# Five buffers for value tiles, table products inside the block loop, a later token row, and another split of the fill steps in a hybrid encoder layer

## The chip, the cores and the metric

The kernel runs on one core of a Trainium2 chip. The metric is device time in microseconds (us) of one execution. The engines are named as in the profile: PE (TensorE, matmuls), DVE (VectorE), ACT (ScalarE), POOL (GpSimd) and SP, whose queue issues every DMA of this kernel. Each engine works through its own list of instructions in order and waits where an operand or a buffer is not ready.

## The reference

One layer of a bidirectional encoder on 1024 tokens of width 1024, fp32. An input projection of the RMS-normed tokens gives latents for a multi-head latent attention (8 heads), q, k and v of a dilated attention (24 heads of 64 in three groups with window and dilation (128,1), (512,4), (2048,16)), two gating inputs and two merge gates:

```
h = rmsnorm(x); proj = h @ w_in
c_q, c_kv, k_rope, z_mla, q_dil, k_dil, v_dil, z_dil, g_mla, g_dil = split(proj)
a_out = mla_attention(rmsnorm(c_q) @ w_uq, rmsnorm(c_kv) @ w_ukv, rope(k_rope))
outs, lses = dilated_group(rope(q_dil), rope(k_dil), v_dil)   # per group
d_out = sum(softmax(lses over the groups) * outs)
y_mla = (a_out * silu(z_mla)) @ w_o_mla;  y_dil = (d_out * silu(z_dil)) @ w_o_dil
x = x + (sigmoid(g_mla + b) * y_mla + sigmoid(g_dil + b) * y_dil) @ w_out
return rmsnorm(x, final_norm_g)
```

## The kernel before

Every product is made in three matmuls, `mm3`: each fp32 operand is split into a high part (`w_h`, a cast on ACT, L150) and the remainder (`w_l`, a subtraction on POOL or DVE, L151), and L144 to L146 add high x high, high x low and low x high. The tokens stay unnormed; the factor 1/rms of each token is multiplied in later, either by partition (`rcol`, a column per 128 tokens) or along the free axis (`R`, a row of 1024 factors that is broadcast to 128 partitions through a DRAM tensor, `s_rs`).

The stages, by the trace:

- 0 to 226 us, in an order that a list scheduler makes: projection of the latents, tables of cosines and sines (`cos_d` and `sin_d` for the dilated heads, tile name `cs_d`), the token factors (`token_factors`: squares, inverse root, `rcol`, and the row `R` by a transpose on PE, L279, and two DMAs), the latents' up-projection (`latents`, whose scaling L357 on DVE comes before PE's transposes L364, whose results ACT empties into `lat_h`, L367, from a ring of two PSUM banks), and the values of the dilated heads (`dil_v`, three groups by two halves, 8 token tiles of 24 matmuls each). `dil_v` takes a tile from PSUM in a high part on ACT (L445) and a low part on DVE (L446) into the SBUF tile `dv_st`, and stores it to `s_dv`; the ring of `dv_st` has three buffers, so the fourth tile waits for the first store to land. Among this runs the loading of up-projection weights: `u_raw`, one buffer, which is cast on ACT into `uq_h` and split on POOL into `uq_l` in two portions, so the second portion's load waits for the first portion's split.
- 226 to 531 us, `blocks`: 16 items of 7 products of 12 matmuls, in an order written out by hand (Strassen-like combinations of half blocks). In each step `x`, operands of the product five places ahead (LEAD) are cast and split, on POOL among others, and each finished item is rotated with `cos_d` and `sin_d` (L549) and stored as q or k of the dilated heads.
- 531 to 828 us, the dilated attention, a hand-written loop over 72 units and some ends (`attention`). Four pairs of heads have 18 units each: 8 units of group 0, 8 of group 1, and 2 *class units* of group 2 (its dilation makes 16 classes of 64 tokens). One pass of the loop is called a tick below: transposes of unit t (L1144, or L1248 for class units), scores of unit t+2 (L1120, L1121; L1231), ACT's cast of the transposed probabilities (L1152) and DVE's low part (L1156), maxima (L1130), exponentials (L1137), and the values of unit t-1 (L1168, L1175; L1262). Twice in a tick `feed(DIL_FEED[g])` adds to a count of owed steps and issues one *fill* step for each whole step owed: a step is three matmuls of 512 columns of other projections (gates and z, 16 tiles in two halves of 8 steps). When a half is complete its epilogue (L728 on DVE, L730 or L734 on ACT, L731 and L732 on POOL, stores to `s_zs` and `s_gt`) and the split of the next weights follow. The keys and queries of a head are loaded (`at_r<-s_dk`, `at_r<-s_dq`) when the units of two heads before are through.
- After each pair, `combine` weighs the three groups by their softmax denominators: a chain of small operations, much of it on POOL (L1410, L1418, L1421, L1422, L1428), then the spreading of the weights by DMA (`at_f<-s_rr`). It runs in the ticks of the next pair, and SP issues these loads ahead of later heads' keys.
- 828 to 1125 us the latent attention, with the rest of the fill; then the output projection.

In a tick the order is: transposes, scores, casts, then the first feed, earlier results, the second feed, values:

```
            do(t, 3)
            do(t + 2, 0)
...
            self.feed(DIL_FEED[g])
            do(t - 2, 6)
            do(t + 2, 2)
            do(t - 2, 7)
...
            self.feed(DIL_FEED[g])
            do(t - 1, 5)
```

Of the kernel before, what the change touches and what calls it, by code (L numbers as in the profile page):

```python
# [10 lines left out]
F32 = mybir.dt.float32  # L11
F32R = mybir.dt.float32r
I32 = mybir.dt.int32
AF = mybir.ActivationFunctionType
ALU = mybir.AluOpType
# [13 lines left out]


FIRST_FEED = 9
DIL_FEED = (1.33, 1.33, 2.3, 1.8)

LAST_JOBS = [(dt, 0) for dt in range(4)] + [(dt + i, half) for dt in (4, 6) for half in range(2) for i in range(2)] + [(dt, 1) for dt in range(4)]
LAST_STEPS = {3: 4, 4: 6, 5: 8, 6: 9, 8: 14, 9: 15, 10: 17, 11: 19, 12: 20}
# [25 lines left out]
class Net:  # L61
# [203 lines left out]
            if half == 0:  # L265
                v.tensor_scalar(out=self.hb, in0=self.hb, scalar1=0.5, scalar2=None, op0=ALU.mult)

    def token_factors(self, xp, pp):

        nc, a = self.nc, self.a  # L270
        ss = xp.tile([128, 8], F32, name="x_ss", bufs=1)
        for t in range(8):
            x = xp.tile([128, D], F32, name="x_in")
            self.dma(x, a["x"][128 * t:128 * t + 128, :])
            nc.scalar.activation(out=x, in_=x, func=AF.Square, accum_out=ss[:, t:t + 1])
        y = self.rsqrt(ss, 1.0 / D, xp, 8)
        nc.vector.tensor_copy(self.rcol, y)
        pt = pp.tile([128, 512], F32, name="pj")
        nc.tensor.transpose(pt[:8, :128], y, self.ident)  # L279
        row = xp.tile([8, 128], F32, name="x_row", bufs=1)  # L280
        nc.vector.tensor_copy(row, pt[:8, :128])
        self.dma(self.rs, row)
        flat = self.rs.rearrange("a b -> (a b)")
        self.dma(self.R, flat.partition_broadcast(128))
# [137 lines left out]
    def dil_v(self, g, quad, tp, pj):  # L422

        nc, a = self.nc, self.a
        w = []
        for kk in range(2):
            raw = self.wp.tile([128, 4, 256], F32, name="w_raw")
            self.dma(raw, a["wv"][g * 2 + quad, kk])
            for k in range(0, 4, 2):
                wp = (self.wp, self.wpx)[kk]  # L430
                h = wp.tile([128, 2, 256], F32R, name="w_h", bufs=4)
                l = wp.tile([128, 2, 256], F32R, name="w_l", bufs=4)
                self.split(raw[:, k:k + 2], h, l, nc.gpsimd)
                w.append((h, l))
        for t in range(8):
            ps = pj.tile([128, 512], F32, name="pj")[:, :256]
            for kc in range(8):
                wh, wl = w[kc // 2]
                sl = slice(128 * t, 128 * t + 128)
                self.mm3(ps, self.hTh[:, kc, sl], self.hTl[:, kc, sl], wh[:, kc % 2], wl[:, kc % 2], kc == 0, kc == 7)  # L440
            pv = ps.rearrange("p (h d) -> p h d", d=64)
            f = self.rcol[:, t:t + 1]
            if g < 2:
                st = tp.tile([128, 4, 2, 64], F32R, name="dv_st")
                nc.scalar.mul(st[:, :, 0], pv, f)  # L445
                nc.vector.scalar_tensor_tensor(out=st[:, :, 1], in0=pv, scalar=f, in1=st[:, :, 0].bitcast(F32), op0=ALU.mult, op1=ALU.subtract)  # L446
                x = slice(quad * 512, quad * 512 + 512)
                if g == 0:
                    dst = self.dv[0][128 * t + 64:128 * t + 192, x]
                else:  # L450

                    dst = self.dv[1].rearrange("(r m) x -> m r x", r=4)[32 * t:32 * t + 32, :, x]
                self.dma(dst, st.rearrange("p h a d -> p (h a d)"))
            else:
                st = tp.tile([128, 4, 64], F32, name="dv_s2")
                nc.scalar.mul(st, pv, f)
                self.dma(self.dv[2][2 * quad:2 * quad + 2, 128 * t:128 * t + 128].rearrange("a t x -> t a x"), st.rearrange("p (a h) d -> p a (h d)", h=2))
# [191 lines left out]
    def blocks(self, items, tp, pp):  # L649

        self.blk, self.opd = {}, {}
        self.raw_pools = (self.wp, tp)
        self.s = [(h, l) for h, l in zip(self.sh, self.sl)]
        places = 7 * len(items)
        steps, ps = {}, {}
        for n in range(2):
            self.block_loads(n, items[n])
        for i in range(4):
            self.dma(self.dq[2][i].rearrange("e c r h (a b) f m -> (e c r) (h a) (b f m)", a=2), self.zero.unsqueeze(1).to_broadcast([128, 4, 512]))
        for j in range(LEAD):  # L660
            self.block_minus(j, items)
            self.block_operand(j, items)
        self.block_minus(LEAD, items)
        with self.tc.manual_schedule():
            for x in range(1, places + 14):
                n, k = divmod(x - 1, 7)
                j = x - 1
                if j < places:
                    if k == 0:
                        ps[n] = {c: pp.tile([128, 512], F32, name=f"st_{c}{n % 2}") for c in "abcd"}  # L670
                        steps[n] = self.block_steps(n, items[n], ps[n], tp)
                    self.block_product(j, ps[n])
                todo = []

                for m, y in ((n, k + 1), (n - 1, k + 8)):
                    if m in steps:
                        todo += steps[m].pop(y, [])
                for f in todo:
                    f()
                self.block_operand(j + LEAD, items)  # L680
                self.block_minus(j + LEAD + 1, items)

                if x == places - 1:
                    self.close_sums()
                    self.open_areas(0)
                    for load in self.items[0][:2]:
                        load()

                if j == places - 9:
                    self.weights_load(0)  # L690
                    self.weights_load(1)
                if j == places - 3:
                    self.weights_split(0)
                if k == 2 and n + 2 < len(items):
                    self.block_loads(n + 2, items[n + 2])
# [875 lines left out]
    def run(self):  # L1571
        tc, nc = self.tc, self.nc
        with ExitStack() as ctx:
# [28 lines left out]
            with tc.tile_pool(name="wpx", reuse_waits="tile", bufs=2, side="right") as self.wpx, tc.tile_pool(name="cosd", reuse_waits="tile", bufs=1, side="right") as dpool, ExitStack() as sums:  # L1602
                with tc.tile_pool(name="pj_a", reuse_waits="tile", bufs=NB_A, space=PSUM) as pj, tc.tile_pool(name="dvp", reuse_waits="tile", bufs=3, side="right") as vp:
                    with tc.tile_pool(name="lp", reuse_waits="tile", bufs=1) as lp, tc.tile_pool(name="pj_l", reuse_waits="tile", bufs=8 - NB_A, space=PSUM) as pl:
                        with tc.tile_pool(name="wl", reuse_waits="tile", bufs=1) as wl, tc.tile_pool(name="xp", reuse_waits="tile", bufs=3) as xp:
                            self.latent_proj(lp, wl, xp, pj)
                            self.tables(xp)
                            self.token_factors(xp, pl)
                            m = cp.tile([128, 896], F32, name="masks")
                            for x, y, n in ((0, 1024, 256), (256, 896, 128), (384, 256, 512)):  # L1610
                                self.dma(m[:, x:x + n], self.a["masks"][:, y:y + n])

                            self.mask0 = m[:, 64:320], m[:, 384:640], m[:, 640:896]
                            self.mask1 = m[:, 128:384], m[:, 0:256]
                        with tc.tile_pool(name="cosm", reuse_waits="tile", bufs=1) as mpool, tc.tile_pool(name="up", reuse_waits="tile", bufs=1) as lp:
                            self.cos_m, self.sin_m = self.table(mpool, "cs_m", 32)
                            self.cos_d, self.sin_d = self.table(dpool, "cs_d", 0)
                            up = self.up_weights(lp)
                            with tc.tile_pool(name="lt", reuse_waits="tile", bufs=2) as tp:
                                self.latents(up, lp, tp, pl)  # L1620
                            self.dil_v(0, 0, vp, pj)
                            self.dil_v(0, 1, vp, pj)
# [4 lines left out]
                    with tc.tile_pool(name="bs", reuse_waits="tile", bufs=1) as tp:  # L1627
                        self.block_sums(sp, tp)
                        self.dil_v(1, 0, vp, pj)
                    for g, quad in ((1, 1), (2, 0), (2, 1)):  # L1630
                        self.dil_v(g, quad, vp, pj)
                    for x in (self.cos_d, self.sin_d):
                        for half in range(2):
                            c = slice(512 * half, 512 * half + 512)
                            nc.gpsimd.tensor_tensor(out=x[:, c], in0=x[:, c], in1=self.R[:, c], op=ALU.mult)
                    for r in (0, S + 64):
                        for p in range(2):
                            self.dma(self.dk[0][:, p, :, :, r:r + 64].rearrange("h c x t -> (c x) h t"), z[:64].rearrange("p (h t) -> p h t", t=64))
# [8 lines left out]
            pp = ctx.enter_context(tc.tile_pool(name="banks", reuse_waits="tile", bufs=1, space=PSUM))  # L1647
# [95 lines left out]
```

## Time and profile before

Three runs took 1252.14, 1256.94 and 1256.76 us, median 1256.76. The profiled execution took 1254.46 us, and its span in the trace is 1252.5 us.

| engine | busy us | share of the span |
|---|---|---|
| PE | 1212.4 | 97% |
| DVE | 730.8 | 58% |
| ACT | 622.0 | 50% |
| POOL | 570.2 | 46% |

A row of PE's waits names what waited (engine, tile, line), what ended it, the sum in us, how often, and the longest. A row of the table by stretches gives for each engine, in the order PE, PEld (weight loads), DVE, ACT and POOL, the busy us and the instructions, then the clock that PE was granted (1.00 is full), the share of the 16 DMA engines, and GB/s. A row of the timeline is start, duration, engine, line, operation, result<-operands, count; in brackets the idle time before it and what ended it. DMA issues have size and median us from issue to landing.

### The profile page before, as it was taken

To read this page: it belongs to the slowest core of one execution; us is meant where nothing else is said; L and a number is where in the kernel's file an instruction comes from. 1 tells how busy PE (TensorE), PEld (TensorE's weight loads), DVE (VectorE), ACT (ScalarE), POOL (GpSimd) and SP (SyncE) were. 2 spreads that over 40 slices of the span, in tenths; PEclk is the share of its full clock that TensorE was granted. 3 is DMA by queue.
4 is the path that set the end of the run, shared out by engine and by line. 5 is a ranking of instruction groups with operands and counts; after the bars stand their busy time and mean duration, and the time that the engine had idled before them with its cause. 6 is when DMAs were issued, how large, how long until landed. Compare 5 with 4: busy or idle time off the path is not lost.

```text
span 1252.5 us, 19486 instructions
## 1 busy us (share of the span) xinstructions
PE 1212.4 (97%) x6909; PEld 1064.5 (85%) x6909; DVE 730.8 (58%) x1304; ACT 622.0 (50%) x1300; POOL 570.2 (46%) x482
## 2 busy tenths in 40 slices
PE   8979999999999999999999999999999999999998
PEld 8979999888888888888888889878878888888886
DVE  7473534467657653345555575647766767759542
ACT  6534345444343344455554666545655656654232
POOL 2352218877777777543464442415521201168322
PEclk9989999999999999999999999899999999999999
DMA  9847589365445642496887898964634445225241
GB/s 333 225 157 283 196 302 317 103 180 156 135 132 165 174 127 100 122 268 197 233 257 200 207 294 212 266 175 116 178 128 119 110 118 135 85 96 182 84 151 51
DMA packets 126416, 221.37 MB, mean 177 GB/s; under 512 B 28072, under 2 KB 60400, under 8 KB 121392
## 3 DMA queue, kind: packets, MB, share of 16 engines
q1 hardware_dynamic: 126320, 220.14, 59.5%
q8 instruction: 54, 0.88, 0.3%
q14 instruction: 42, 0.34, 0.1%
HBM read 149.24 MB, written 70.85 MB: 176 GB/s over the span
## 4 chain that ended last, share of the span: by engine, by line
PE 75%; DMA 11%; DVE 4%; ACT 4%; issue 3%; POOL 1%; SPq 1%; ACTq 0%; POOLq 0%; DVEq 0%
PE bank L145 5%; PE bank L144 5%; PE bank L146 5%; PE pj L145 4%; PE bank L871 4%; PE pj L144 4%; PE pj L146 4%; DMA at_r<-s_dk 3%; PE st_a L144 2%; PE st_a L145 2%; PE st_d L145 2%; PE st_c L145 2%; PE st_d L146 2%; PE st_a L146 2%; PE st_c L146 2%
## 5 line engine op out<-in xcount | busy, mean ns | idle before, releaser
L151 POOL TENSOR_TENSOR w_l<-w_raw,w_h 128x512 fp32r<-128x512 f32 x188 | 247.5, 1330 | 276.7 <-ACT w_h L150 218.1
L150 ACT CAST w_h<-w_raw 128x512 fp32r<-128x512 f32 x188 | 112.6, 621 | 110.1 <-POOL w_raw L495 92.7
L144 PE MATMUL bank<-at_r,w_h 128*128 128x512 f32 x344 | 142.8, 415 | 0.0
L879 DVE TENSOR_TENSOR at_r<-bank,at_r 128x512 fp32r<-128x512 f32 x128 | 88.0, 688 | 84.5 <-ACT at_r L873 84.2
L145 PE MATMUL bank<-at_r,w_h 128*128 128x512 f32 x344 | 136.6, 397 | 0.6 <-POOL at_r L151 0.6
L146 PE MATMUL bank<-at_r,w_l 128*128 128x512 f32 x344 | 136.7, 397 | 0.0
L873 ACT CAST at_r<-bank 128x512 fp32r<-128x512 f32 x128 | 74.9, 586 | 72.5 <-PE bank L871 71.9
L145 PE MATMUL pj<-w_l,at_r 128*128 128x256 f32 x384 | 109.7, 286 | 0.0
L146 PE MATMUL pj<-w_h,at_r 128*128 128x256 f32 x384 | 109.6, 285 | 0.0
L144 PE MATMUL pj<-w_h,at_r 128*128 128x256 f32 x384 | 109.5, 285 | 0.0
L1137 ACT ACTIVATE at_f<-at_f,at_f 128x256 f32<-128x256 f32 x128 | 64.1, 502 | 52.1 <-DVE at_f L1130 51.8
L1156 DVE TENSOR_TENSOR at_r<-bank,at_r 128x512 fp32r<-128x512 f32 x64 | 43.9, 686 | 70.4 <-ACT at_r L1152 70.3
L495 POOL TENSOR_TENSOR w_raw<-w_raw 128x512 f32<-128x512 f32 x64 | 82.8, 1294 | 0.1
L871 PE MATMUL bank<-consts,at_f 128*128 128x128 f32 x512 | 77.2, 273 | 1.7 <-ACT at_f L863 1.1
L146 PEld LDWEIGHTS bank<-at_r,w_l 128*128 128x128 f32 x344 | 65.7, 191 | 14.9
L146 PEld LDWEIGHTS pj<-w_h,at_r 128*128 128x128 f32 x384 | 74.2, 193 | 1.0
L145 PEld LDWEIGHTS pj<-w_l,at_r 128*128 128x128 f32 x384 | 74.3, 193 | 0.7
L144 PEld LDWEIGHTS pj<-w_h,at_r 128*128 128x128 f32 x384 | 74.2, 193 | 0.7
L145 PEld LDWEIGHTS bank<-at_r,w_h 128*128 128x128 f32 x344 | 65.9, 192 | 9.9 <-POOL at_r L151 1.0
L144 PEld LDWEIGHTS bank<-at_r,w_h 128*128 128x128 f32 x344 | 65.8, 191 | 9.2
L895 PE MATMUL bank<-at_r,at_r 128*128 128x256 f32 x256 | 67.7, 285 | 1.3 <-ACT at_r L873 1.3
L896 PE MATMUL bank<-at_r,at_r 128*128 128x256 f32 x256 | 67.5, 285 | 0.9 <-DVE at_r L879 0.9
(321 smaller groups left out, 3325.3 us busy)
## 6 DMA issues: line engine op xcount, KB each, us to landing
w_raw<-wt SPq DMA_DIRECT2D x48, 512.0 KB, 3.7
at_r<-s_dq SPq DMA_DIRECT2D x32, 512.0 KB, 7.3
s_dk<-dq_st SPq DMA_DIRECT2D x80, 128.0 KB, 2.4
s_dv<-dv_st SPq DMA_DIRECT2D x32, 256.0 KB, 3.0
s_dq<-dq_st SPq DMA_DIRECT2D x64, 128.0 KB, 2.4
zt<-s_gt SPq DMA_DIRECT2D x32, 256.0 KB, 4.5
w_raw<-wv SPq DMA_DIRECT2D x12, 512.0 KB, 5.8
at_r<-s_dk SPq DMA_DIRECT2D x8, 576.0 KB, 11.3
```

The source lines that it names most:

```text
L144: mm(out, lh, rh, start=start, stop=False, skip_group_check=skip)
L145: mm(out, lh, rl, start=False, stop=False, skip_group_check=skip)
L146: return mm(out, ll, rh, start=False, stop=stop, skip_group_check=skip)
L150: self.nc.scalar.copy(out=h, in_=raw)
L151: sub.tensor_tensor(out=l, in0=raw, in1=h.bitcast(F32), op=ALU.subtract)
L495: self.nc.gpsimd.tensor_tensor(out=b[out], in0=b[x], in1=b[y], op=ALU.subtract)
L871: self.nc.tensor.transpose(pt[:, o:o + 128], self.P[k, b][:, 128 * kc:128 * kc + 128], self.ident)
L873: self.nc.scalar.copy(out=h, in_=pt)
L879: self.nc.vector.tensor_tensor(out=l, in0=pt, in1=h.bitcast(F32), op=ALU.subtract)
L895: mm(out, vv[:, kc], ph[:, x], start=kc == 0, stop=False)
L896: mm(out, vv[:, kc], pl[:, x], start=False, stop=kc == 7)
L1137: nc.scalar.activation(out=p, in_=p, func=AF.Exp, scale=-1.0, bias=nm, accum_out=den)
```

## The change

It has four parts: `dv_st` gets five buffers; the token row is made by a function of its own, called after the block sums and one pass of values of group 1; the four POOL multiplications of `cos_d` and `sin_d` by `R` move from the region of the scheduler into the steps x = 2 to 5 of `blocks`; and the owed steps per call of `feed` become 1.17 for groups 0 and 1 (1.33 before) and 3.5 for class units (2.3).

```diff
-DIL_FEED = (1.33, 1.33, 2.3, 1.8)
+DIL_FEED = (1.17, 1.17, 3.5, 1.8)
...
-    def token_factors(self, xp, pp):
+    def token_factors(self, xp):
...
         nc.vector.tensor_copy(self.rcol, y)
+
+    def token_row(self, tp, pp):
+
+        nc = self.nc
         pt = pp.tile([128, 512], F32, name="pj")
-        nc.tensor.transpose(pt[:8, :128], y, self.ident)
-        row = xp.tile([8, 128], F32, name="x_row", bufs=1)
+        nc.tensor.transpose(pt[:8, :128], self.rcol, self.ident)
+        row = tp.tile([8, 128], F32, name="x_row", bufs=1)
         nc.vector.tensor_copy(row, pt[:8, :128])
         self.dma(self.rs, row)
...
-                st = tp.tile([128, 4, 2, 64], F32R, name="dv_st")
+                st = tp.tile([128, 4, 2, 64], F32R, name="dv_st", bufs=5)
...
+                if x in (2, 3, 4, 5):
+                    y, c = (self.cos_d, self.sin_d)[x // 2 - 1], slice(512 * (x % 2), 512 * (x % 2) + 512)
+                    self.nc.gpsimd.tensor_tensor(out=y[:, c], in0=y[:, c], in1=self.R[:, c], op=ALU.mult)
...
                         self.dil_v(1, 0, vp, pj)
+                    self.token_row(vp, pj)
                     for g, quad in ((1, 1), (2, 0), (2, 1)):
                         self.dil_v(g, quad, vp, pj)
-                    for x in (self.cos_d, self.sin_d):
-                        for half in range(2):
-                            c = slice(512 * half, 512 * half + 512)
-                            nc.gpsimd.tensor_tensor(out=x[:, c], in0=x[:, c], in1=self.R[:, c], op=ALU.mult)
```

The scheduler puts the start of the program into another order. The first place is ACT's list around the first value tiles (`dv_st`), the casts of the up-projection weights (`uq_h`) and the emptying of the latents' transposes (`lat_h`). Before:

```order
L262 ACTIVATE x_junk,lat_ss<-pj 128x128
L445 ACTIVATE dv_st<-pj,rcol 128x4x64 x5
L150 CAST uq_h<-u_raw 128x768
L445 ACTIVATE dv_st<-pj,rcol 128x4x64
L367 ACTIVATE lat_h<-pj,consts 128x512 x2
L445 ACTIVATE dv_st<-pj,rcol 128x4x64
L150 CAST w_h<-w_raw 128x512 x3
L150 CAST uq_h<-u_raw 128x768
L367 ACTIVATE lat_h<-pj,consts 128x512
```

And of the change, where L449 and L371 are the former L445 and L367:

```order
L262 ACTIVATE x_junk,lat_ss<-pj 128x128
L449 ACTIVATE dv_st<-pj,rcol 128x4x64 x3
L150 CAST uq_h<-u_raw 128x768
L449 ACTIVATE dv_st<-pj,rcol 128x4x64 x2
L150 CAST uq_h<-u_raw 128x768
L371 ACTIVATE lat_h<-pj,consts 128x512 x2
L449 ACTIVATE dv_st<-pj,rcol 128x4x64
L371 ACTIVATE lat_h<-pj,consts 128x512
```

Both casts of `uq_h` now stand ahead of the first `lat_h`, where one did before. On PE the token row's transpose has left this region, and the latents' first transposes stand 27 matmuls earlier in its list; on SP the first load of `u_raw` stands ahead of the first stores of `dv_st`, where it stood behind three.

The second place is POOL's list in the dilated attention, the combine of the second pair (`at_512_f`, `at_768_f`) among the fill's work (`zt`, `w_l`). Before:

```order
L1410 TENSOR_TENSOR at_512_f<-at_512_f,at_768_f 16x128 x3
L731 TENSOR_TENSOR zt<-zt 128x512
L732 TENSOR_TENSOR zt<-zt 128x512
L151 TENSOR_TENSOR w_l<-w_raw,w_h 128x512 x2
L1418 TENSOR_TENSOR at_768_f<-at_512_f,at_768_f 16x128
L1418 TENSOR_TENSOR at_768_f<-at_512_f,at_768_f 16x2x16x4
L1418 TENSOR_TENSOR at_768_f<-at_512_f,at_768_f 16x2x4x16
```

And of the change (L1417, L1425 and L1435 are the former L1410, L1418 and L1428, L738 and L739 the former L731 and L732):

```order
L1417 TENSOR_TENSOR at_512_f<-at_512_f,at_768_f 16x128 x3
L1425 TENSOR_TENSOR at_768_f<-at_512_f,at_768_f 16x128
L1425 TENSOR_TENSOR at_768_f<-at_512_f,at_768_f 16x2x16x4
L1425 TENSOR_TENSOR at_768_f<-at_512_f,at_768_f 16x2x4x16
L1428 TENSOR_TENSOR at_768_f<-at_768_f 16x128 x2
L1429 TENSOR_TENSOR at_768_f<-at_768_f 16x128
L738 TENSOR_TENSOR zt<-zt 128x512
L739 TENSOR_TENSOR zt<-zt 128x512
L1435 TENSOR_TENSOR at_512_f<-at_512_f,at_768_f 16x128 x3
L151 TENSOR_TENSOR w_l<-w_raw,w_h 128x512 x2
```

The epilogue's two operations stand further back in the chain, and the weights' split behind it.

More of the change, by code (lines that the diff above doesn't have):

```diff
@@ L1607, in run @@
                             self.tables(xp)
-                            self.token_factors(xp, pl)
+                            self.token_factors(xp)
                             m = cp.tile([128, 896], F32, name="masks")
```

## The prediction

> **What bounds the kernel now.** I first read TensorE's (PE's) waits over the whole span, largest first.
>
> ```profile
> span 1252.5 us, 19486 instructions
> PE pj L364 <- DVE lat L357: 7.5, 2, 6.8
> PE right L1120 <- DMA at_r<-s_dk: 5.9, 3, 2.6
> PE pj L144 <- ACT wl_h L150: 5.8, 1, 5.8
> PE pj L279 <- DVE rs_y L209: 1.9, 1, 1.9
> PE left L1175 <- DVE at_r L1156: 1.6, 2, 1.3
> ```
>
> PE is the bound: no single wait is over 8 us in 1252.5. So a change can pay only in these waits and in what they do to the clock. The third (the program's start) is not touched. Then I read the stretches (PE busy first, the granted clock after POOL's column).
>
> ```profile
> 50.00:75.00 25.00, 15.61 (x118) 14.91 (x116) 17.47 (x75) 4.88 (x13) 6.78 (x5) 0.84 0.60 166
> 226.00:531.00 305.00, 304.12 (x1342) 251.90 (x1343) 171.19 (x272) 127.29 (x241) 219.60 (x180) 1.00 0.49 140
> 71.30:77.30 6.00, 5.24 (x24) 4.95 (x25) 6.00 (x19) 1.26 (x2) 1.69 (x1) 0.50 0.00 0
> 671.30:674.70 3.40, 3.40 (x10) 2.64 (x9) 0.72 (x4) 1.09 (x4) 0.00 (x0) 0.50 0.98 221
> 743.80:747.20 3.40, 3.40 (x18) 2.89 (x19) 2.05 (x7) 1.36 (x4) 0.00 (x0) 1.00 1.10 270
> 804.40:811.20 6.80, 6.80 (x24) 5.93 (x24) 4.31 (x9) 2.31 (x6) 1.92 (x3) 0.50 1.00 201
> ```
>
> After some waits the clock is 0.50 for 3.4 to 6.8 us; half of that is lost beside the wait (3.0 us in the third row, 1.7 in the fourth, 3.4 in the last). The block products (226 to 531) leave PE 0.9 us idle. So only the start around 50 to 77 and the dilated attention (531 to 828) can move.
>
> **The five buffers and the late token row (start).**
>
> ```profile
> 55.86 1.18 SPq L140 DMA_DIRECT2D s_dv<-dv_st  x2
> ...
> 63.71 1.10 ACT L445 ACTIVATE dv_st<-pj,rcol 128x256 fp32r<-128x256 f32 x2 [8.11 <-DMA s_dv<-dv_st]
> 67.14 0.83 ACT L150 CAST uq_h<-u_raw 128x768 fp32r<-128x768 f32 x1 [2.34 <-DMA u_raw<-wuq]
> ...
> 64.22 0.48 DVE L446 SCALAR_TENSOR_TENSOR dv_st<-pj,rcol,dv_st 128x256 fp32r<-128x256 f32 x1 [6.23 <-ACT dv_st L445]
> 67.45 2.52 DVE L353 TENSOR_TENSOR rs_y<-rs_y,rcol 128x4 f32<-128x4 f32 x4
> ...
> 66.21 4.96 POOL L1635 TENSOR_TENSOR cs_d<-cs_d,at_f 128x512 f32<-128x512 f32 x4 [19.52 <-DVE rs_u L208]
> 71.14 1.86 POOL L151 TENSOR_TENSOR uq_l<-u_raw,uq_h 128x768 fp32r<-128x768 f32 x1
> ...
> 64.05 0.28 PE L145 MATMUL pj<-w_l,at_r 128*128 128x256 f32 x1
> 64.17 0.28 PE L146 MATMUL pj<-w_h,at_r 128*128 128x256 f32 x1
> 71.38 0.69 PE L364 MATMUL pj<-consts,lat 128*128 128x128 f32 x2 [6.81 <-DVE lat L357]
> 73.39 0.69 PE L364 MATMUL pj<-consts,lat 128*128 128x128 f32 x2 [0.69 <-DVE lat L357]
> ```
>
> The fourth value tile waits 8.11 us on ACT for a store issued at 55.86; DVE waits 6.23 behind it, and the latents' scaling (L357), on which PE's transposes wait, comes after that. With five buffers neither waits for a store so early. DVE's own chain then ends about 6.2 + 2.2 us sooner (L353 took 0.63 each while POOL multiplied the tables; that work leaves), near 61 to 63. PE reaches its transposes at 64.4 - 2.05 (the token row's transpose with its wait is gone) - 27 x 0.12 (so many matmuls fewer stand ahead of them) = 59.1. There remain 2 to 4 us.
>
> But the new order puts both casts uq_h on ACT ahead of L371 (the old L367), which empties the transposes' two banks; PE's second pair of transposes waits for it. The first of the two weight loads now takes the queue place of the store issued at 55.86, so it lands near 64. Cast 0.83, split on POOL 1.86, then the second load into the same buffer, which landed 4.8 us after issue before, 2 at best if alone (my bound), 2.8 taken: 69.5. Cast 0.83, L371 twice 0.7: PE goes on at about 71.8, against 71.38 before, with 22 matmuls more behind it. Gain: 22 x 0.12 + 0.69 (the wait at 73.39 is gone) - 0.4 = **2.9 us**, the half clock staying. Bounds: 0 if the load lands 3 us later. If ACT's wait vanishes, the waits 1.9 + 7.5 and the 3.0 of half clock go less the 2 to 4 that remain: -9 at most.
>
> **The four table multiplications.** POOL does them in products 2 to 5: 4 x 1.24 us = 5.0. POOL is busy 219.6 of 305 there, 85 us free, and its operands are made five products (13.6 us, 305 / 112 each) ahead. That lead covers them: 0. Without the lead up to 2.0 us (5.0 less POOL's free 28% of four products). The row's broadcast is issued three passes of value tiles (576 matmuls of 0.12 us) ahead of its first use, so it can't be late.
>
> **The feed.** A step is three matmuls of 512 columns:
>
> ```profile
> 552.52 0.40 PE L144 MATMUL bank<-at_r,w_h 128*128 128x512 f32 x1
> ...
> 553.90 0.27 PE L1144 MATMUL bank<-consts,at_f 128*128 128x128 f32 x1
> ...
> 599.16 0.39 PE L1120 MATMUL right<-at_r,at_r 128*128 128x256 f32 x1 [1.39 <-DMA at_r<-s_dk]
> 670.50 0.36 PE L1120 MATMUL right<-at_r,at_r 128*128 128x256 f32 x1 [1.92 <-DMA at_r<-s_dk]
> 743.68 0.36 PE L1120 MATMUL right<-at_r,at_r 128*128 128x256 f32 x1 [2.62 <-DMA at_r<-s_dk]
> ```
>
> Two steps in 1.38 us, 0.69 each. Head ticks get 2.34 steps in place of 2.66, class ticks 7.0 in place of 4.6; over the stage 230 and 229, so the work itself is 0. By adding the feed up tick for tick, at a pair's first class tick the fill is now 5 to 7 steps behind, and repaid only afterwards. That tick's scores (L1120) wait for the next pair's keys *ahead of* its feed, so PE comes to this wait earlier and the loads must be earlier too. First wait: the loads start at tick 13 and ticks 13 to 15 lose one step: **+0.7**. Second and third: the loads follow the combine's chain on POOL.
>
> ```profile
> 627.84 1.43 POOL L1410 TENSOR_TENSOR at_f<-at_f,at_f 16x128 f32<-16x128 f32 x3 [4.26 <-DVE at_f L1408]
> 632.45 1.43 POOL L1418 TENSOR_TENSOR at_f<-at_f,at_f 16x128 f32<-16x128 f32 x3 [3.17 <-ACT at_f L1413]
> ...
> 702.11 1.41 POOL L1410 TENSOR_TENSOR at_f<-at_f,at_f 16x128 f32<-16x128 f32 x3 [8.61 <-DVE at_f L1408]
> ...
> 706.10 2.55 POOL L151 TENSOR_TENSOR w_l<-w_raw,w_h 128x512 fp32r<-128x512 f32 x2
> 708.60 1.42 POOL L1418 TENSOR_TENSOR at_f<-at_f,at_f 16x128 f32<-16x128 f32 x3
> ```
>
> Second: 3.5 steps fewer lie between (2.4 us), but two of the fill's multiplications move out of the chain (2.6 at the 1.28 each of the w_l row above, less 1.1 in which POOL would wait anyway: 1.5) and a 512 KB weight load moves behind the keys (2.4 us at the 221 GB/s above; as transfers overlap, 1 taken): **0**, bounds -2 to +2.4. Third: four steps fewer (2.8); the chain from L1410 to L1418 falls from 6.5 to 4.6, but two fill operations come in later (+1.5), so 0.4 is saved: **+2.4**. A wait of 1.92 was followed by half clock and one of 2.62 was not; at 5 I take half of a 3.4 stretch's loss: **+0.8**. Bounds of the three waits together: -2.6 (third gone) to +8.
>
> [...]
>
> The tail: PE's wait at L1175 comes from a fill's epilogue in front of a head's exponentials:
>
> ```profile
> 799.81 0.69 DVE L728 TENSOR_TENSOR zt<-bank,at_f 128x512 f32<-128x512 f32 x1 [1.96 <-DMA s_gt<-zt]
> ...
> 542.18 0.60 PE L1144 MATMUL bank<-consts,at_f 128*128 128x128 f32 x4
> 588.31 0.60 PE L1144 MATMUL bank<-consts,at_f 128*128 128x128 f32 x4
> ...
> 543.16 0.59 ACT L1152 CAST at_r<-bank 128x512 fp32r<-128x512 f32 x1 [1.29 <-POOL area L1282]
> 592.31 0.59 ACT L1152 CAST at_r<-bank 128x512 fp32r<-128x512 f32 x1
> ...
> 803.08 0.56 ACT L1152 CAST at_r<-bank 128x512 fp32r<-128x512 f32 x1
> 805.86 0.58 ACT L1152 CAST at_r<-bank 128x512 fp32r<-128x512 f32 x1
> ```
>
> That epilogue (step 208) moves from a head tick into a class tick, but step 200's moves to where it was; of 1.6 + 3.4 us I take half: **-2.5**, bounds -5 to 0. Last, ACT's cast, DVE's low part and maxima and ACT's exponentials follow each other from tick to tick: the casts are 2.78 us apart at the closest here, over the first pair's 14 head ticks (592.31 - 543.16) / 14 = 3.51, PE's transposes 3.30. Head ticks get 0.22 us shorter; the class ticks let ACT catch up. I take **+1**, bounds 0 to +5.
>
> **Sum:** -2.9 + 0 + 0.7 + 0 + 2.4 + 0.8 - 2.5 + 1 = -0.5. On the profiled execution's own 1254.46 (2 us around its span) that is 1254.0; that execution lay 2.3 under the runs' median of 1256.76, so 1256.3. 0.5% is 6.3 us, about what a measurement of this kernel can tell from no change.
>
> **Rivals.**
> *A, the start is freed:* the second weight load lands early and ACT does not hold PE, so the half clock does not come: -9 in place of -2.9, sum -6.6; if the fill's tail wait goes whole, -9.1: 1248 to 1250. For it: POOL and the queue lose the tables and the 512 KB broadcast there. Against: the order has both casts ahead of L371. 0.28.
> *B, slower, ACT becomes the pace of head ticks:* 3.51 per tick in the first pair was already above PE's 3.30. Where the cast's rhythm decides in all 64 head ticks, the 0.22 taken from each comes back as waiting and the class ticks' 14 us of extra work are not covered: +14 x 0.8 - 2.9 = +8.3, 1265. It decides once the casts lag 3.5 us, where PE waits. Against: from the second pair on the casts mostly follow PE at once. 0.15.
> *C, slower, the keys:* all three waits grow by 2.4 and each draws a half-clock stretch (1.7; one does already): 7.2 + 3.4 - 2.9 - 2.5 + 1 = +6.2, 1263. It decides where the DMA engines stay full for the whole load (0.98 and 1.10 of them in the rows above). 0.10.
> *D, the buffers do nothing* (ACT's new wait eats all): start 0, sum +2.4, 1259; inside the forecast.
> Forecast and D: 0.47.
>
> **Numbers.** Faster 0.28, same 0.47, slower 0.25. The bounds of the unknown costs reach from about -14 to +15; 8 in 10 lie between 1244 and 1268. The forecast's own range is 1250 to 1262.
>
> **What would show it.** Start: ACT without a wait for s_dv<-dv_st before 70, PE's wait ahead of the second pair of transposes, the clock 0.50 until 77 (A: none). Blocks: PE idle under 1 us. Waits on at_r<-s_dk: about 2, 2 and 5 us in place of 1.4, 1.9 and 2.6. The wait on L1156 near 800 smaller. B would show as many small PE waits on L1137 and L1152, C as 0.50 stretches after the second and third key waits. It is wrong if the sum of 531 to 828 gets shorter by over 3 us, or the blocks longer by over 2.

## The result, and the profile after

The changed kernel is slower by 0.64%: ratio 1.0064 of the mean times, 95% interval 1.0045 to 1.0083, medians 1260.51 against 1251.29 us over 15 runs each; one run of the changed kernel, slow at 3103.8 us, is left out of the ratio. Forecast was no change that can be told (1256.3, within 1244 to 1268). That 1260.51 lies in this range is luck: the forecast was -0.5 us from a median of 1256.76, and in these runs the kernel before had 1251.29. The two profiled executions differ by 4.3 us of span, about half of the 8 us of the ratio: the one of before was a long run for its kernel (1254.46, median 1251.29), the changed one a short one (1258.7, median 1260.51). So the traces are read for the places of the loss, and the runs for its size.

PE's waits in the changed kernel, to be laid beside those of before (L1127, L1151, L368 and L460 are the former L1120, L1144, L364 and L456):

```profile
PE right L1127 <- DMA at_r<-s_dk: 12.0, 3, 5.8
PE pj L144 <- ACT wl_h L150: 5.8, 1, 5.8
PE pj L368 <- DVE lat_l L372: 5.5, 1, 5.5
PE bank L1151 <- ACT at_f L1144: 2.5, 10, 0.8
PE pj L144 <- ACT dv_s L460: 2.4, 1, 2.4
```

The waits for the keys doubled, from 5.9 to 12.0. The two waits at the start (7.5 on L357 and 1.9 on the token row) became one of 5.5, a new one of 2.4 appeared, and the tail's waits (L1175, 1.6) went. All this is one trace of each kernel, and waits differ from one execution to the next: in the six traces shown here or below that have the old feed and the scores in their old place (before, e2, e6, e7, e8, e9) the key waits sum to 2.9 to 5.9 us. The 12.0 of the changed kernel, and the 9.6 of e1 below, stand clear of that; the 5.9 of before is its upper end. Stretches of the changed kernel (columns as in the tables before; the clock stands after POOL's column):

```profile
67.70:74.50 6.80, 3.87 (x18) 3.74 (x19) 3.19 (x6) 3.42 (x6) 1.82 (x1) 0.50 0.47 145
217.90:221.30 3.40, 3.40 (x18) 3.40 (x17) 1.27 (x2) 2.82 (x8) 3.24 (x3) 0.50 0.39 117
596.70:600.10 3.40, 3.40 (x10) 2.92 (x11) 0.78 (x4) 1.09 (x4) 1.56 (x2) 0.51 0.99 226
668.40:671.80 3.40, 3.40 (x10) 2.65 (x9) 1.79 (x6) 0.39 (x1) 0.00 (x0) 0.50 1.09 302
740.10:746.90 6.80, 3.48 (x10) 3.01 (x11) 3.03 (x9) 2.37 (x6) 0.00 (x0) 0.50 1.04 296
```

The clock now halves at all three key waits (before: after the second alone; the third stretch of the changed kernel begins 3.3 us before its wait ends, and PE is busy for 3.48 of its 6.80 us), after the new wait at 217, no more near 804, and for 6.8 rather than 10.2 us at the start (67.7 to 74.5, before 67.1 to 77.4). The three key waits in the timeline of the changed kernel:

```profile
596.70 0.56 PE L1127 MATMUL right<-at_r,at_r 128*128 128x256 f32 x1 [3.34 <-DMA at_r<-s_dk]
667.55 0.36 PE L1127 MATMUL right<-at_r,at_r 128*128 128x256 f32 x1 [2.77 <-DMA at_r<-s_dk]
743.42 0.55 PE L1127 MATMUL right<-at_r,at_r 128*128 128x256 f32 x1 [5.84 <-DMA at_r<-s_dk]
```

The start, PE and ACT in the changed kernel:

```profile
70.63 1.12 PE L368 MATMUL pj<-consts,lat 128*128 128x128 f32 x4 [5.48 <-DVE lat_l L372]
216.60 0.39 PE L144 MATMUL pj<-w_h,at_r 128*128 128x256 f32 x1 [2.38 <-ACT dv_s L460]
...
68.38 0.83 ACT L150 CAST uq_h<-u_raw 128x768 fp32r<-128x768 f32 x1 [4.86 <-DMA u_raw<-wuq]
69.11 1.26 ACT L371 ACTIVATE lat_h<-pj,consts 128x512 fp32r<-128x512 f32 x2
215.56 0.62 ACT L150 CAST s_h<-y 128x512 fp32r<-128x512 f32 x1 [3.57 <-POOL y L479]
216.08 0.47 ACT L460 ACTIVATE dv_s<-pj,rcol 128x256 f32<-128x256 f32 x1
...
213.02 1.28 POOL L499 TENSOR_TENSOR w_raw<-w_raw 128x512 f32<-128x512 f32 x1
214.27 1.25 POOL L479 TENSOR_TENSOR y<-y,y 128x512 f32<-128x512 f32 x1
```

At 70.63 the chain is the one foretold: load, cast, L371, transposes. At 216 ACT's list has a cast of the block sums, which waits for POOL (behind a weight subtraction for the blocks), ahead of the emptying of a value tile, and PE waits for that tile's bank. Matmuls done by 80 us (PE's count, first before and then changed):

```profile
0.00:80.00 80.00, 64.62 (x390) 63.09 (x391) 51.09 (x132) 44.11 (x98) 25.43 (x23) 0.94 0.76 243
...
0.00:80.00 80.00, 68.70 (x423) 67.24 (x424) 52.56 (x137) 47.36 (x103) 24.89 (x21) 0.96 0.80 249
```

33 matmuls more, 4.0 us at 0.12 each. The block products' first matmul, however, and the first transpose of the latent attention (before, then changed) are

```profile
226.88 0.50 PE L144 MATMUL st_a<-at_r,w_h 128*128 128x512 f32 x1 [0.96 <-ACT dv_s L456]
836.49 0.27 PE L871 MATMUL bank<-consts,at_f 128*128 128x128 f32 x1
...
226.82 0.40 PE L144 MATMUL st_a<-at_r,w_h 128*128 128x512 f32 x1
842.56 0.27 PE L878 MATMUL bank<-consts,at_f 128*128 128x128 f32 x1
```

What the start gained, the wait at 216.60 (2.4) and its half clock (half of 3.4) took back. The products' last matmul starts at 531.43 and 531.26, so in these two traces the whole loss lies in the dilated stage, which is 6.2 us longer; what follows it is 1.8 us shorter (416.0 before, 414.2 after), which leaves the 4.3 of the spans.

### The profile page after: what moved, and what is told of

Read it like the earlier page. It is cut to its first block, busy times and chain, and to the rows that moved or that the text cites. A ratio compares the mean times of both kernels' runs of the same rounds, so it can differ in the third digit from the quotient of the medians.

```text
span 1256.8 us, 19468 instructions
## 1 busy us (share of the span) xinstructions
PE 1214.8 (97%) x6909; PEld 1065.7 (85%) x6909; DVE 720.3 (57%) x1304; ACT 622.0 (49%) x1300; POOL 568.2 (45%) x482
## 4 chain that ended last, share of the span: by engine, by line
PE 72%; DMA 13%; POOL 4%; DVE 4%; ACT 3%; issue 3%; SPq 1%; ACTq 0%; POOLq 0%; DVEq 0%
PE bank L145 6%; PE bank L144 6%; PE bank L146 6%; PE bank L878 4%; DMA at_r<-s_dk 3%; PE st_a L145 2%; PE st_c L145 2%; PE st_d L145 2%; PE st_a L144 2%; PE st_d L144 2%; PE st_c L144 2%; PE st_a L146 2%; PE st_d L146 2%; PE st_c L146 2%; PE bank L903 2%
## 5 line engine op out<-in xcount | busy, mean ns | idle before, releaser
L1144 ACT ACTIVATE at_f<-at_f,at_f 128x256 f32<-128x256 f32 x128 | 64.1, 502 | 59.4 <-DVE at_f L1137 59.1
L878 PE MATMUL bank<-consts,at_f 128*128 128x128 f32 x512 | 77.4, 273 | 1.5 <-ACT at_f L870 1.1
L144 PEld LDWEIGHTS pj<-w_h,at_r 128*128 128x128 f32 x384 | 74.5, 194 | 3.4 <-ACT dv_s L460 2.6
```

The costliest lines, as they stand in the source:

```text
L144: mm(out, lh, rh, start=start, stop=False, skip_group_check=skip)
L878: self.nc.tensor.transpose(pt[:, o:o + 128], self.P[k, b][:, 128 * kc:128 * kc + 128], self.ident)
L1144: nc.scalar.activation(out=p, in_=p, func=AF.Exp, scale=-1.0, bias=nm, accum_out=den)
```

## The experiments

All ratios are to the kernel before, measured on the same chip in turn. "Half clock" is worked out from the mean granted clock c that each run lists: (1 - c) times the run's time is what the reduced clock cost it at most (stretches in which PE waited anyway are in it too), and the mean over the runs is given.

| kernel | ratio (95%) | half clock us |
|---|---|---|
| changed kernel | 1.0064 (1.0045 to 1.0083) | 14.7 |
| e1 feed's numbers alone | 1.0034 (1.0014 to 1.0053) | 12.2 |
| e2 all but the feed | 1.0023 (1.0004 to 1.0043) | 13.1 |
| e3 feed the other way | 1.0016 (0.9991 to 1.0041) | 14.8 |
| e4 changed, feed ahead of scores | 0.9938 (0.9918 to 0.9958) | 7.1 |
| e5 before, feed ahead of scores | 0.9948 (0.9924 to 0.9972) | 10.9 |
| e6 five buffers alone | 0.9990 (0.9963 to 1.0016) | 13.6 |
| e7 e2, group 2's values on DVE | 1.0000 (0.9983 to 1.0017) | 13.8 |
| e8 e2, two weight buffers | 0.9963 (0.9950 to 0.9977) | 14.2 |
| e9 row and tables alone | 0.9991 (0.9966 to 1.0016) | 12.2 |
| e10 e4 and two weight buffers | 0.9906 (0.9877 to 0.9936) | 7.6 |
| e11 before, five buffers, new feed, ahead | 0.9945 (0.9920 to 0.9969) | 7.8 |
| e12 changed, both feeds ahead | 0.9935 (0.9913 to 0.9957) | 8.0 |

The kernel before lost in this way 12.2 us beside e1 to e4, 13.5 beside e5 to e8 and 14.1 beside e9 to e12, each on another chip (29 to 33 runs on each).

**e1, the feed alone.**

```diff
-DIL_FEED = (1.33, 1.33, 2.3, 1.8)
+DIL_FEED = (1.17, 1.17, 3.5, 1.8)
```

> Only the numbers of the feed are changed, the rest is the kernel before. Keys theory (the scores of a pair's first class tick wait for the next pair's keys ahead of that tick's feed, and the fill now lies 5 to 7 steps behind there): waits on at_r<-s_dk of 11 to 13 us in sum, as in the changed kernel (12.0), against 5.9 before, and 1.004 to 1.009 of the time before. Pace theory (ACT and DVE can't follow the shorter head ticks): the same ratio, but the loss in many waits on the exponentials and the cast, over 5 us in sum, and the key waits under 8. Start theory (what was lost was lost ahead of 226 us): a ratio of 0.999 to 1.002.

1.0034. PE's waits:

```profile
PE right L1120 <- DMA at_r<-s_dk: 9.6, 3, 4.5
...
PE bank L1144 <- ACT at_f L1137: 2.6, 10, 0.8
```

Key waits 9.6 against 5.9 before (11 to 13 were expected), the pace of ACT and DVE 2.6 against 1.7. The ratio, too, is a little under the 1.004 to 1.009 of the keys theory, which is borne out in the main; the pace theory, which wanted over 5 us there and under 8 for the keys, falls. Over the 12 runs the half clock costs no more than in the kernel before on the same chip (12.2 both), so the loss here is waiting.

**e2, everything but the feed.** The changed kernel with the old `DIL_FEED`.

> The changed kernel with the old numbers of the feed: five buffers, late token row, table products in the blocks. Keys theory: the dilated stage is as before (key waits near 5.9 us), and the block products start at 226.8 us as in both kernels, since the 4 us gained by 80 us are lost again at 214 to 221: ratio 0.997 to 1.001. Start theory: slower, 1.004 or more.

1.0023, a little above the expected 0.997 to 1.001, below the 1.004 of the start theory; its interval holds the nearest value of both. With e1's 1.0034 it makes up 1.0057 of the 1.0064. Where its 0.23% is lost isn't shown: in its trace the blocks start 1.5 us later than before, the dilated stage is 1.3 us shorter, and the part behind it, which lasts between 412 and 420 us in the fourteen traces, is 3.5 us longer. Its trace has the start's two waits as the changed kernel has them:

```profile
PE pj L368 <- DVE lat_l L372: 5.3, 1, 5.3
...
PE right L1127 <- DMA at_r<-s_dk: 2.9, 2, 1.6
PE pj L144 <- ACT dv_s L460: 2.3, 1, 2.3
```

**e3, the feed the other way.**

```diff
-DIL_FEED = (1.33, 1.33, 2.3, 1.8)
+DIL_FEED = (1.45, 1.45, 1.34, 1.8)
```

> The kernel before with the feed moved the other way: 1.45 steps per call in head ticks, 1.34 in class ticks, so that the fill is 3 to 5 steps ahead of before at the first class tick. Keys theory: the key waits shrink from 5.9 to 0 to 3 us, ratio 0.993 to 0.999. Pace theory: head ticks get 0.17 us longer, small waits go, ratio 0.994 to 0.999, but the key waits stay between 4 and 6. If longer head ticks also hold back the loads (they are issued by the ticks themselves), the waits stay and the ratio is 1.000.

1.0016, with no clear sign. Two of the key waits did not shrink but grew, and the third was gone:

```profile
604.41 0.35 PE L1120 MATMUL right<-at_r,at_r 128*128 128x256 f32 x1 [3.06 <-DMA at_r<-s_dk]
...
676.08 0.36 PE L1120 MATMUL right<-at_r,at_r 128*128 128x256 f32 x1 [3.64 <-DMA at_r<-s_dk]
```

The simple form of the keys theory (more fill ahead of the wait, less waiting) misses here. In this trace the first keys were issued at 590.4 and landed at 604.3, 13.9 us (worked out from its SP row and PE's start), where they took 11.7 before. Why they took longer isn't shown; which other transfers (weights, gates) fall into the load moves with the fill as well. So more fill ahead of this wait, by the numbers of the feed alone, did not shorten it.

**e4, the changed kernel with the first feed of class ticks ahead of the scores.**

```diff
             do(t, 3)
+            if g == 2:
+                self.feed(DIL_FEED[g])
             do(t + 2, 0)
...
-            self.feed(DIL_FEED[g])
+            if g != 2:
+                self.feed(DIL_FEED[g])
             do(t - 2, 6)
```

> The changed kernel, but in class ticks the first feed (3 or 4 steps, 2.1 to 2.8 us) is issued ahead of the scores that wait for the keys, in place of behind them. Keys theory: each of the three waits is covered by 2.1 to 2.8 us, their sum falls from 12.0 to 4 to 6, and the time to 0.999 to 1.004 of the kernel before. If the loads of the keys are held by something that PE does later (their issue follows the units), they land later by as much and the waits stay at 12.

0.9938, better than the expected 0.999 to 1.004: 1.25% under the changed kernel by the two ratios. The remaining key waits in the timeline:

```profile
594.93 0.39 PE L1127 MATMUL right<-at_r,at_r 128*128 128x256 f32 x1 [1.71 <-DMA at_r<-s_dk]
...
732.15 0.36 PE L1127 MATMUL right<-at_r,at_r 128*128 128x256 f32 x1 [2.28 <-DMA at_r<-s_dk]
```

4.0 in sum, as the keys theory said. In this trace no half clock follows them (the matmuls of 512 columns behind them take 0.39 to 0.40 us, against 0.63 in the half clock of the changed kernel), and over all runs the half clock costs 7.1 us where the changed kernel has 14.7. So of the 15.5 us between the two kernels' mean times (1245.4 and 1260.9) about half is waiting (8.0 less for the keys, by one trace each) and up to half is the clock (7.6). The wait for the keys is filled with matmuls that stood behind it.

**e5, the kernel before with that edit alone.** The same diff on the kernel before.

> The kernel before, with its own numbers of the feed, and only the first feed of class ticks (2 or 3 steps, 1.4 to 2.1 us) issued ahead of the scores that wait for the keys. Keys theory: the waits of 1.4, 1.9 and 2.6 us are covered but for 0 to 1 us, key waits of 0 to 2 in sum, and with fewer stretches of half clock 0.993 to 0.998 of the time before. If what made the changed kernel with the feed ahead fast (0.994) is the larger feed of the class ticks, which 1.4 to 2.1 us can't replace: 0.998 to 1.001.

0.9948, as expected, with nothing left of the waits but

```profile
PE right L1120 <- DMA at_r<-s_dk: 0.2, 1, 0.2
```

So the order of feed and scores in two ticks of a pair gains where the four parts of the change together lose, and needs none of them.

**e6, the five buffers alone.** `bufs=5` for `dv_st` in the kernel before.

> The kernel before with five buffers for the value tiles and nothing else; token row and table products stay early. If the buffers alone lift the first wait: ACT does not wait for s_dv<-dv_st before 70 us, PE's wait on L357 falls from 7.5 to 2 to 4 us, the rest as before, 0.996 to 1.000. If the row and the tables matter as much (POOL slows DVE's chain, the row's broadcast delays the weights), the wait stays above 5 and the ratio is 0.999 to 1.001.

0.999, no difference that can be told over 12 runs. The profiled execution, the shortest of the 12, has the start at its best: no wait on L357, a granted clock of 1.00 in each stretch from 50 to 230 us, and the block products start 7.1 us earlier than before:

```profile
219.74 0.50 PE L144 MATMUL st_a<-at_r,w_h 128*128 128x512 f32 x1 [0.84 <-ACT dv_s L456]
```

e11 below, which has the same start (the instructions up to the block products stand on every engine in the order of the kernel before), begins them early too, without a wait on L357, and with a mean clock of 0.994 in its trace (0.990 in that of before):

```profile
221.31 0.50 PE L144 MATMUL st_a<-at_r,w_h 128*128 128x512 f32 x1 [1.82 <-ACT dv_s L456]
```

Four traces with three buffers and that order (before, e1, e3, e5) begin them at 225.8 to 227.3. So both traces with the buffers alone show a gain of 4 to 8 us that reaches the blocks. That it reaches the end isn't shown: the traced run of e6 lasted 1245.5 us, but the other eleven lie between 1248.7 and 1263.6, and where they lose it is open.

**e7, the values of group 2 scaled on DVE** (L460, `nc.scalar.mul` to `nc.vector.tensor_scalar`) in e2.

> The changed kernel with the old numbers of the feed, and the scaling of group 2's value tiles (L460) moved from ACT to DVE, so that it does not stand behind the casts of the block sums. If the wait at 214 to 217 us (2.4 us and a stretch of half clock after it) is only ACT's order: it goes, the block products start 3 to 4 us earlier than with the same kernel without this, near 224, ratio 0.996 to 1.000. If the sums themselves hold the blocks, the products start near 227 to 228 all the same and the ratio is 1.000 to 1.004.

1.000 against e2's 1.0023, with intervals that overlap. The wait did not go, it only changed its engine, and the blocks start at 226.05, between the two values expected:

```profile
220.19 0.39 PE L144 MATMUL pj<-w_h,at_r 128*128 128x256 f32 x1 [1.90 <-DVE dv_s L460]
```

DVE's list holds the same block sums' low parts, which wait for ACT's casts. The wait is that of the sums in the scheduler's order, not of ACT.

**e8, two buffers for the up-projection weights** (`u_raw`, `bufs=2`) in e2.

> The changed kernel with the old numbers of the feed and two buffers for the up-projection weights, so that the second load does not wait for the first portion's split. If the wait of 5.3 us ahead of the second pair of transposes is that chain (load, cast, split, load, cast): it falls under 2.5 us and the half clock after it goes, PE is 4 to 6 us further at 80 us; the end gains only what the wait at 217 us leaves, ratio 0.997 to 1.001. If the queue is what is late, the wait stays at 4 to 5 us.

0.9963, better than e2's 1.0023 by more than the intervals, but not for the reason given: the wait grew,

```profile
75.16 1.12 PE L368 MATMUL pj<-consts,lat 128*128 128x128 f32 x4 [7.57 <-DVE lat_l L372]
...
72.68 1.05 ACT L150 CAST ukv_h<-u_raw 128x1024 fp32r<-128x1024 f32 x1 [4.55 <-DMA u_raw<-wukv]
```

since the scheduler now put a third cast, `ukv_h`, ahead of L371 as well. The wait at 217 is gone, and the blocks start at 224.46 (e2's at 228.37). But one start differs by more than that from execution to execution: with the order of the changed kernel the blocks begin at 226.8 (changed), 228.4 (e2), 224.6 (e4) and 230.7 (e12). Half clock is no less (14.2), so the gain is in waiting; where, isn't shown.

**e9, token row and tables alone** (three buffers, old feed).

> The kernel before with the late token row and the table products in the blocks, value tiles with three buffers as before, old feed. The start with all three parts measured 1.0023, five buffers alone 0.999. If the row and the tables cause the new order that loses at 217 us: the wait near 217 is there, the wait at the start is between 3 and 9 us, ratio 1.002 to 1.006. If only both together make that order: 0.998 to 1.002 and no wait of over 1.5 us between 200 and 226.

0.9991. The two waits of the new order are there with three buffers:

```profile
PE pj L368 <- DVE lat_l L372: 5.2, 1, 5.2
...
PE pj L144 <- ACT dv_s L460: 1.8, 1, 1.8
```

Its instructions up to the block products stand in the order of the changed kernel on every engine, those of e6 in the order of the kernel before. So the new order comes from the row and the tables, not from the buffers. It costs the early start that the buffers alone have in e6 and e11 (blocks at 219.7 and 221.3, with the new order at 224.6 to 230.7 in five traces); that it costs time in the end isn't shown (e9 0.9966 to 1.0016, e2 1.0004 to 1.0043).

**e10, e4 and e8 together; e11, the new feed ahead of the scores on the kernel before with five buffers; e12, both feeds of the class ticks ahead** (`self.feed(2 * DIL_FEED[g])` in e4's place, none later).

> The changed kernel with the feed of class ticks ahead of the scores (0.9938) and two buffers for the up-projection weights (0.9963 with the old feed, against 1.0023 without). If the two gains add: 0.986 to 0.990. If the gain of the second is only in when the clock halves, they don't: 0.992 to 0.996.

> The kernel before with five buffers, the changed numbers of the feed, and the class ticks' first feed ahead of the scores; token row and tables stay early. If the row and the tables are a loss of 0.3%: 0.988 to 0.993. If they are not: 0.993 to 0.996 as in the changed kernel with the feed ahead.

> The changed kernel with both feeds of a class tick (7 steps, 4.8 us) ahead of its scores. Keys theory: the key waits, 4.0 us in sum with one feed ahead, fall under 1, ratio 0.990 to 0.994. Against it: scores and maxima come 2.4 us later, so the exponentials of the next heads may be late; then waits on L1144 or L1182 over 3 us in place of the keys, and 0.994 to 0.999.

e10 has the lowest ratio, 0.9906, 0.94% under the kernel before, between the two ranges expected; its interval still overlaps e4's, so that the two gains add isn't shown. In its trace there is no wait between 205 and 231, and the blocks start at 221.0. e11 gives 0.9945: with the scores moved, the late row and the tables make no difference to the time that can be told. e12 gives 0.9935, its key waits are gone altogether, and

```profile
PE bank L1151 <- ACT at_f L1144: 3.3, 10, 1.1
```

rises from 2.3 in e4. That is the trade foreseen in kind, but not shown to come from the second feed: with one feed ahead the same wait is 4.1 in e10 and 3.3 in e11. There is no net gain over e4.

## Why the prediction was wrong, by its own steps

**The bound** was right as far as the loss and the gains are placed: they lie in PE's waits at the start and in the dilated stage, and in the half clock behind them.

**Five buffers and late row** (-2.9): up to 80 us the mechanism was as forecast. PE went on at 70.63 (71.8 forecast) behind the second cast of `uq_h`, ACT had no early wait for a store, and the gain by 80 us was 4.0. (The second weight load, taken at 2.8 us, took 3.6, from its issue at 64.72 to the cast at 68.38; no run shows it alone, and the bound of 2 was the author's assumption: the shortest load of 512 KB of weights took 3.2 us to land, one of 78 KB of constants 1.9.) The first step that failed is the unsaid one that this gain reaches the end. The prediction looked at the order around 50 to 80 us and not at 200 to 226, where the same rescheduling put a cast of the sums ahead of a value tile; 2.4 us and 1.7 of half clock brought it to 0. That was rival D's number, for another reason. e7 shows that this second wait belongs to the order of the sums, e9 that the row and tables bring it, and e6 and e11 that the buffers without them free the start: the prediction took the late row for a part of the gain, and in the traces the row and the tables undo it.

**Table products in the blocks** (0): right; products 304.6 us before, 304.4 after. What moving them out of the start does to its order (e9, with the row) was not considered.

**Keys** (+0.7, 0, +2.4, +0.8; 3.9 in sum): the mechanism was right, and this is the term that was mis-sized, the second step that failed. The waits grew by 1.95, 0.85 and 3.22 us, 6.0 in sum. Half clock came with each, and PE was busy in 3.4, 3.4 and 3.5 us of it against 3.4 before; half of the difference is another 3.4. That is 9.4. PE came 4.4, 3.8 and 3.5 us earlier to the three waits (worked out from the starts less the waits, 596.70 - 3.34 against 599.16 - 1.39 for the first), but the keys less: their issue, in SP's rows of before and then of the changed kernel,

```profile
587.46 0.58 SPq L140 DMA_DIRECT2D at_r<-s_dk  x1
657.66 0.33 SPq L140 DMA_DIRECT2D at_r<-s_dk  x1
730.57 0.38 SPq L140 DMA_DIRECT2D at_r<-s_dk  x1
...
583.77 0.59 SPq L140 DMA_DIRECT2D at_r<-s_dk  x1
655.40 0.57 SPq L140 DMA_DIRECT2D at_r<-s_dk  x1
728.53 0.41 SPq L140 DMA_DIRECT2D at_r<-s_dk  x1
```

came 3.7, 2.3 and 2.0 us earlier. So the lead of the loads fell by 0.7, 1.5 and 1.4, 3.7 in sum, where the prediction had 0.7, 0 and 2.4, 3.1: nearly its size. What it had at nothing is the loads' own duration: from issue until PE went on passed 12.93, 12.15 and 14.89 us rather than 11.70, 12.84 and 13.11, which adds 2.3 in sum. Why the first and the third took longer isn't shown. And the clock: it priced one further stretch by half, +0.8, and in the trace it is +3.4. Over all runs that part is smaller: the half clock is 14.7 in the changed kernel, and 12.2 to 14.1 in the kernel before by chip.

**Tail** (-2.5): the wait went as argued, with its half clock: 1.6 + 3.4, the bound of -5. More traces bear it out: that wait (L1175, or L1182 as its new number) is 1.6 to 3.0 us in all seven with the old feed and at most 0.4 in all six with the new. **Pace** (+1): L1151 2.5 against 1.7, so +0.8.

With the sizes measured the sum is 0 + 0 + 9.4 - 5 + 0.8 = +5.2 for these terms, against -0.5; the stage is 6.2 longer in the trace, and the runs' ratio says 8.0. The rest, e2's loss among it, isn't placed. **Rivals:** C, priced at +6.2 with a chance of 0.10, is nearest to what happened, with the start's gain lost besides, though the second wait grew by 0.85 and not by 2.4. Its condition (DMA engines full for the whole load) doesn't tell the kernels apart. The first and third load, before and then changed:

```profile
587.46:599.16 11.70, 10.31 (x74) 9.34 (x72) 7.00 (x13) 6.07 (x14) 6.92 (x6) 1.00 1.00 259
730.57:743.68 13.11, 10.35 (x74) 9.23 (x72) 9.53 (x18) 7.26 (x17) 4.52 (x5) 1.00 1.02 251
...
583.77:596.70 12.93, 9.59 (x71) 8.71 (x69) 7.59 (x12) 6.10 (x13) 5.33 (x5) 1.00 1.02 234
728.53:743.42 14.89, 8.74 (x60) 7.50 (x60) 8.00 (x14) 6.67 (x15) 5.63 (x5) 0.89 1.02 252
```

The share is 1.00 and 1.02 before, 1.02 and 1.02 after. B fell with e1. A did not occur in the changed kernel; its freed start is that of e6 and e11. Two slips in the working changed nothing: the lower bounds add up to -16.6, not about -14 (-9, -2.6, -5), and PE was busy 5.24 of the 6.00 us in the third row of the stretches, so half clock cost 2.6 there and not 3.0.

What the prediction had in hand and didn't turn around: it had written that the scores wait *ahead of* their tick's feed, and that the change moves work behind that wait. e4 and e5 are that sentence, reversed.

## What to carry to other kernels

Filler work only covers a wait that stands behind it in the engine's list (here, moved across, it brought the key waits from 12.0 to 4.0 us in e4 and from 5.9 to 0.2 in e5): before giving a step more filler, see on which side of its wait the filler is issued; moving it across was worth 0.5% on the kernel before and 1.25% on the changed one, re-dividing it between steps cost 0.3% one way and gained nothing that can be told the other. A local gain in a scheduled prologue is to be followed to the next place where that prologue meets another chain, since moving a part of it can re-sort the rest (e9), while more buffers alone did not (e6). One trace gives a wait of this size only to within a few us, so it is to be compared over several. And here a key wait of 2.77 us or more was followed by a stretch of half clock in seven of seven cases, one of 1.92 to 2.62 in four of seven: it should be priced with that.

## What the runs showed of the hardware

In the traces of the kernel before and of the changed kernel every stretch of half clock (granted 0.50) that ended inside the program was a multiple of 3.41 us: six of 3.41, three of 6.83, one of 10.24. Which wait draws one isn't set by its length alone: 1.92 us did and 2.62 did not in the kernel before, 3.34, 2.77 and 5.84 all did in the changed one, and in e4 waits of 1.71 and 2.28 did not. Of the 18 key waits in the traces of before, the changed kernel, e1, e3, e4, e5, e10 and e11, all seven of 2.77 us or more had half clock begin in them or within about 1.5 us behind them, four of the seven from 1.92 to 2.62 had, and none of the four shorter ones (0.18 to 1.71); where it came, the matmuls of 512 columns took 0.63 us, elsewhere 0.39 to 0.40.

The mean granted clock of a run carries a large part of the scatter: in e6, runs at 0.986 took 1258 to 1264 us and runs at 0.993 and 0.994 took 1245 to 1249. The four kernels with the new feed ahead of the scores (e4, e10, e11, e12) lost 7 to 8 us to the clock where all others lost 11 to 15; in e4 that is 7.6 less than in the changed kernel, about as much as its key waits fell (8.0).
